# A chain of layers on one core: weight splits in halves and held back at norms, and a state-space stage whose inputs, skip term and Gelu are arranged anew

## The chip, the cores and the metric

The kernel runs on one core of a Trainium2 chip. The metric is the time on the device in microseconds (us), the median of several runs.

## What is computed

Two blocks of layers over 256 tokens of width 1024, all in float32. The first block has two layers: a mixer (a short convolution, then a dilated-window attention with rotary positions), a squared-ReLU MLP, and a gated projection of a side input ("ple"). The second block has two layers: a SwiGLU FFN ("ffn1"), a mixer (a state-space layer "S5", then a three-branch sparse attention), and a second SwiGLU FFN ("ffn2"); keys and values ("kv") for the sparse attention come from the first layer's output. Every part begins with an RMS norm. The state-space layer is the part that the change speaks of most:

```python
_, _, x_re, x_im = lax.associative_scan(combine, (la_re, la_im, bu_re, bu_im), axis=1)
y = (jnp.einsum('bsgp,ghp->bsgh', x_re, c_re) - jnp.einsum('bsgp,ghp->bsgh', x_im, c_im)
     + d_skip * ug)
y = jax.nn.gelu(y.reshape(bsz, seq, D_MODEL))
return y * jax.nn.sigmoid(y @ w_glu)
```

Here `ug` is the normed input in 64 groups of 16 channels, and the state of a group has 64 complex numbers.

## The kernel before

All activations lie transposed, with channels on the 128 partitions and the 256 tokens along the free axis, as 8 slices of 128 channels (`h0` to `h3` hold two each). The weights stream from memory in pieces of 128x2048 float32 (`raw`, 1 MB). A float32 product is made of three matmuls (`mm3`, L333 to L335): ScalarE copies the weights to a rounded high part (`whi`, L267), VectorE subtracts it from them (`wlo`, L271), and TensorE adds up high*high, low*high and high*low. Activations are split the same way (`xh` on ScalarE, `xl` on VectorE). A piece is split in two instructions of 128x1024 on either engine.

`piece` hands out the pieces in the order of a plan. Each call splits up to the piece `ahead` = 3 places on and loads three more. Whole tiles of the pool `ring`, three each of `raw`, `whi` and `wlo`, hold them.

A norm is not waited for: TensorE begins the layer's first pieces on the unscaled input (times the gain), one slice of channels after the other as `h` is written, three pieces at a time. Meanwhile the steps of the norm (`norm_at`, `norm_step`, a list `todo`) run: the mean of squares by a matmul, its power -0.5 (`rmean`, `rcol`), a diagonal `dg`, and a matmul of `dg` with ones (`norm_bc`, L509) whose result ScalarE copies to `R` (L511), the factors along the free axis. The results of the first pieces are multiplied by `R` when they are read (`e0`, L516). With three pieces under way, a fourth one, D, is the next that TensorE begins after them. `when_scaled` and the list `late` hold back what needs `R`; a scheduler sets the rest of the order, except that code under `in_order` is tied to the place where it is written.

The S5 stage (L1130 to L1310) goes by a written sequence, `S5_SEQ`: `r` puts the input rows in a grouped layout, `w` makes the state inputs of a quarter of the groups, `c` is the recurrence of a quarter (products on VectorE and GpSimd, a scan L1223 on VectorE, a rotation back, the states `sX` L1230), `t` and `o` apply two further tables (`to`, the short-range taps, and `wo`, the states), `R` turns half of the results back into channel slices and splits them, `K` (`skip`) multiplies the skip input `XG` by `R` on GpSimd (L1254, 8 instructions). The tables were computed in the background of earlier layers (`s5_taps`, `s5_tables`). ScalarE has already scaled `XG` by the skip weights (L1279). The result of `t` and `o` is copied to `UP` (L1163); at `R` VectorE adds `XG` to the transposed result (L1268), and ScalarE applies Gelu (L1272). After it come the matmuls of `w_glu`, a sigmoid (L1298), a product and the sum with `h` (L1299, L1300). Four pieces of weights in and after the stage (`BY_POOL`) have their low parts made on GpSimd (L269) instead of VectorE.

Of the kernel before, what the change touches and what calls it, by code (L numbers as in the profile page):

```python
# [10 lines left out]
F32 = mybir.dt.float32  # L11
# [6 lines left out]
D = 1024  # L18
# [30 lines left out]
SC_HEAD = SC_D + KT  # L49
# [6 lines left out]
S5_SEQ = "r0 r1 w0 r2 w1 r3 c0 w2 t0 c1 o0 w3 t1 t2 T o1 c2 t3 K o2 c3 R0 o3 R1 S"  # L56
# [143 lines left out]

BY_POOL = {S5_AT + S5_N + i for i in range(4)}
# [9 lines left out]
IN_ORDER = {E.DVE, E.Activation, E.Pool, E.PE}  # L211


class Ker:
    def __init__(self, ctx, tc, a):
# [13 lines left out]
        self.by_pool = BY_POOL  # L229
# [3 lines left out]
    def load(self, i):  # L233
        nc = self.nc
        while self.n_load < min(i, len(PLAN)):
            n, e = self.n_load, PLAN[self.n_load]
            if e[0] == "s5":

                m = (n - S5_AT) % 3
                t = self.ring.tile([128, NP_], F32R if m else F32, name=("raw", "whi", "wlo")[m])  # L240
                t = t.bitcast(F32) if m else t
                nc.sync.dma_start(t, self.s5w[e[1:]])
# [14 lines left out]
    def split(self, i):  # L257
        nc = self.nc
        while self.n_split < min(i, len(PLAN)):
            n = self.n_split  # L260
            assert PLAN[n][0] != "s5"
            self.load(n + 1)
            r = self.raw.pop(n)
            hi = self.ring.tile([128, NP_], F32R, name="whi")
            lo = self.ring.tile([128, NP_], F32R, name="wlo")
            for c in (slice(i, i + 1024) for i in range(0, NP_, 1024)):
                nc.scalar.activation(hi[:, c], r[:, c], AF.Copy)  # L267
                if n in self.by_pool:
                    nc.gpsimd.tensor_tensor(lo[:, c], r[:, c], hi[:, c].bitcast(F32), op=OP.subtract)  # L269
                else:  # L270
                    nc.vector.tensor_sub(lo[:, c], r[:, c], hi[:, c].bitcast(F32))  # L271
            self.spl[n] = (hi, lo)
            self.n_split += 1

    def piece(self, *want, ahead=3):
# [3 lines left out]
        if 0 <= d < S5_N:  # L279
# [3 lines left out]
            self.split(S5_AT + S5_N + max(0, (d - 3) // 3))  # L283
            self.n_use += 1
            return self.raw.pop(i)
        self.split(min(i + ahead, self.cap))
        self.load(i + ahead + 3 if d >= 0 or i + ahead < S5_AT else min(S5_AT + 3 * (i + ahead - S5_AT) + 3, S5_AT + 9))
# [8 lines left out]
    def step(self):  # L296
# [3 lines left out]
        while self.credit >= 1.0:  # L300
# [20 lines left out]

    def flush(self):
        self.credit = 0.0
        while self.bg:
            self.step()
# [11 lines left out]
    def cols_open(self, *want, ahead=3, ps="acc"):  # L337
        wh, wl = (w.rearrange("p (k c) -> p k c", k=KT) for w in self.piece("cols", *want, ahead=ahead))
        return self.psum(ps).rearrange("p (o t) -> p o t", o=2), wh, wl

    def cols_part(self, x, a, ks):
        acc, wh, wl = a
        for k in ks:
            for o in range(2):
                s = slice(128 * o, 128 * o + 128)
                self.mm3(acc[:, o], wh[:, k, s], wl[:, k, s], x[0][k], x[1][k],
# [1516 lines left out]
```

## Time and profile before

| | |
|---|---|
| median of 3 runs | 1875.27 us (1873.52 to 1877.62) |
| the profiled execution | 1871.9 us, its span 1870.1 us, mean granted TensorE clock 0.989 |
| busy | TensorE 97%, VectorE 69%, ScalarE 50%, GpSimd 25% |
| DMA | 344.68 MB, 184 GB/s on average |

PE is TensorE, ACT ScalarE, DVE VectorE, POOL GpSimd, SP the queue of the loads. The span is the time from the first to the last instruction of the core in the profiled execution. A line such as `L509` is line 509 of the kernel before. The granted clock is TensorE's share of full speed; it has two levels, 2.4 GHz (1.00) and 1.2 GHz (0.50), so a mean between them tells how long the lower one held.

### The profile page before, as it was taken

To read this page: it belongs to the slowest core of one execution; us is meant where nothing else is said; L and a number is where in the kernel's file an instruction comes from. 1 tells how busy PE (TensorE), PEld (TensorE's weight loads), DVE (VectorE), ACT (ScalarE), POOL (GpSimd) and SP (SyncE) were. 2 spreads that over 40 slices of the span, in tenths; PEclk is the share of its full clock that TensorE was granted. 3 is DMA by queue.
4 is the path that set the end of the run, shared out by engine and by line. 5 is a ranking of instruction groups with operands and counts; after the bars stand their busy time and mean duration, and the time that the engine had idled before them with its cause. 6 is when DMAs were issued, how large, how long until landed. Compare 5 with 4: busy or idle time off the path is not lost.

```text
span 1870.1 us, 35822 instructions
## 1 busy us (share of the span) xinstructions
PE 1817.1 (97%) x15244; PEld 1792.0 (96%) x15244; DVE 1281.1 (69%) x1633; ACT 942.3 (50%) x1442; POOL 468.5 (25%) x392
## 2 busy tenths in 40 slices
PE   8999999999999999999999779999999999999999
PEld 8999999999999999999999779999999999899999
DVE  6889887888776867778555566555785556875554
ACT  4365556555444555466443455444565445764442
POOL 2120012564652311112010442101243113421110
PEclk9999999999999999999999979999999999999999
DMA  6455666443343576666555734755455453445452
GB/s 253 181 187 209 220 223 219 161 152 142 136 144 127 198 236 227 219 207 254 188 186 187 291 128 172 263 185 186 174 187 200 173 183 118 65 161 181 181 180 90
DMA packets 78927, 344.68 MB, mean 184 GB/s; under 512 B 8022, under 2 KB 34378, under 8 KB 41392
## 3 DMA queue, kind: packets, MB, share of 16 engines
q1 hardware_dynamic: 77616, 339.30, 52.4%
q0 software_dynamic: 1008, 2.91, 0.4%
q8 instruction: 119, 1.95, 0.4%
q14 instruction: 40, 0.33, 0.1%
q10 hardware_dynamic: 144, 0.20, 0.0%
HBM read 328.71 MB, written 17.86 MB: 185 GB/s over the span
## 4 chain that ended last, share of the span: by engine, by line
PE 81%; DVE 7%; POOL 4%; issue 3%; ACT 2%; DMA 1%; SPq 0%; POOLq 0%; ACTq 0%; DVEq 0%
PE acc L334 16%; PE acc L335 16%; PE acc L333 16%; PE big L333 9%; PE big L334 9%; PE big L335 9%; DVE wlo L271 3%; POOL qks L736 2%; POOL qkt L739 1%; PE acc L1690 1%; POOL qkc L738 1%; ACT whi L267 1%; DMA bias<-zb 1%; PE big L1673 1%; PE misc L485 0%
## 5 line engine op out<-in xcount | busy, mean ns | idle before, releaser
L267 ACT ACTIVATE whi<-raw 128x1024 fp32r<-128x1024 f32 x558 | 559.8, 1051 | 599.8 <-issue 360.9
L271 DVE TENSOR_TENSOR wlo<-raw,whi 128x1024 fp32r<-128x1024 f32 x550 | 698.7, 1305 | 224.5 <-ACT whi L267 223.9
L334 PE MATMUL acc<-xl,whi 128*128 128x256 f32 x2096 | 595.7, 285 | 3.6 <-DVE xl L460 3.0
L333 PE MATMUL acc<-xh,whi 128*128 128x256 f32 x2096 | 594.5, 285 | 4.5 <-ACT whi L410 2.3
L335 PE MATMUL acc<-xh,wlo 128*128 128x256 f32 x2096 | 595.8, 285 | 3.0 <-DVE wlo L411 2.8
L333 PEld LDWEIGHTS acc<-xh,whi 128*128 128x128 f32 x2096 | 403.2, 193 | 6.4 <-ACT whi L410 2.7
L335 PEld LDWEIGHTS acc<-xh,wlo 128*128 128x128 f32 x2096 | 403.8, 193 | 5.3 <-DVE wlo L411 3.4
L334 PEld LDWEIGHTS acc<-xl,whi 128*128 128x128 f32 x2096 | 403.8, 193 | 4.8 <-DVE xl L460 3.4
L334 PE MATMUL big<-hl,whi 128*128 128x256 f32 x1216 | 343.6, 283 | 0.0
L335 PE MATMUL big<-hh,wlo 128*128 128x256 f32 x1216 | 343.2, 283 | 0.0
L333 PE MATMUL big<-hh,whi 128*128 128x256 f32 x1216 | 341.1, 284 | 0.0
L334 PEld LDWEIGHTS big<-hl,whi 128*128 128x128 f32 x1216 | 232.8, 191 | 0.5 <-issue 0.5
L335 PEld LDWEIGHTS big<-hh,wlo 128*128 128x128 f32 x1216 | 232.7, 191 | 0.2 <-issue 0.2
L333 PEld LDWEIGHTS big<-hh,whi 128*128 128x128 f32 x1216 | 231.0, 191 | 1.9 <-issue 1.9
L855 POOL TENSOR_TENSOR e<-e,R 128x512 f32<-128x512 f32 x44 | 80.6, 1833 | 524.5 <-ACT e L854 524.5
L335 PE MATMUL acc<-yh,wlo 128*128 128x256 f32 x720 | 204.1, 285 | 1.2 <-DVE wlo L271 1.0
L334 PE MATMUL acc<-yl,whi 128*128 128x256 f32 x720 | 204.1, 286 | 1.0 <-DVE yl L460 0.6
L333 PE MATMUL acc<-yh,whi 128*128 128x256 f32 x720 | 203.0, 286 | 0.8 <-ACT yh L410 0.5
L334 PEld LDWEIGHTS acc<-yl,whi 128*128 128x128 f32 x720 | 138.7, 193 | 2.0 <-DVE yl L460 1.3
L335 PEld LDWEIGHTS acc<-yh,wlo 128*128 128x128 f32 x720 | 138.9, 193 | 1.7 <-DVE wlo L271 1.2
L333 PEld LDWEIGHTS acc<-yh,whi 128*128 128x128 f32 x720 | 138.1, 194 | 2.2 <-ACT yh L410 1.3
L516 DVE TENSOR_TENSOR e<-acc,R 128x512 f32<-128x512 f32 x54 | 36.9, 689 | 84.4 <-PE acc L335 84.1
(440 smaller groups left out, 2592.4 us busy)
## 6 DMA issues: line engine op xcount, KB each, us to landing
raw<-in_wst SPq DMA_DIRECT2D x277, 1024.0 KB, 4.9
s5wo<-b SPq DMA_DIRECT2D x8, 512.0 KB, 5.7
s5wi<-wi SPq DMA_DIRECT2D x16, 256.0 KB, 3.7
s5to<-s5k SPq DMA_DIRECT2D x32, 128.0 KB, 4.5
bias<-zb SPq DMA_DIRECT2D x16, 256.0 KB, 4.5
cbt<-zb SPq DMA_DIRECT2D x4, 900.0 KB, 6.5
raw<-s5to SPq DMA_DIRECT2D x3, 1024.0 KB, 4.8
raw<-in_wst SPq DMA_DIRECT2D x4, 512.0 KB, 7.9
```

What stands on the lines that cost most here:

```text
L267: nc.scalar.activation(hi[:, c], r[:, c], AF.Copy)
L271: nc.vector.tensor_sub(lo[:, c], r[:, c], hi[:, c].bitcast(F32))
L333: mm(out, lh, rh, start=first, stop=False, skip_group_check=True)
L334: mm(out, lh, rl, start=False, stop=False, skip_group_check=True)
L335: mm(out, ll, rh, start=False, stop=last, skip_group_check=True)
L516: self.nc.vector.tensor_tensor(t, acc, self.bc2(self.R), op=OP.mult)
L736: nc.gpsimd.tensor_tensor(s, s, bc(self.rS), op=OP.mult)
L738: nc.gpsimd.tensor_tensor(c, t[:32], bc(self.rC), op=OP.mult)
L739: nc.gpsimd.tensor_tensor(t[:32], c, s, op=OP.add)
L855: nc.gpsimd.tensor_tensor(T[i], T[i], self.bc2(self.R), op=OP.mult)
L1673: nc.tensor.transpose(tp[:, 128 * n:128 * n + 128], blocks[4 * i + n], self.ident)
L1690: nc.tensor.matmul(o[:, dst], w, t[lp][:, e, b, src], start=False, stop=(b == 1 and kb == 1 and i == 2), skip_group_check=True)
```

## The change

It has four parts.

1. **Halves.** `whi` and `wlo` become pairs of 128x1024 tiles with a buffer each, six of either (`Halves`), where there were three of 128x2048. Either half can be split and released by itself. `rows` goes over the halves one after the other.
2. **Ordered splits at norms.** While fewer than four steps of a norm are left in `todo`, and the next two pieces are split, `piece` does not split and load further. It puts that work on `late`, and it is done, tied to its place by `in_order`, when `norm_bc` has issued `R`. Background work (`step`) also waits while a norm has steps left.
3. **The S5 stage.** `XG` has a tile of its own instead of one in the pool that the FFN before uses. The skip weights are added to the diagonal of the taps in the background work, so `XG`, scaled or multiplied by `R`, isn't needed at the end: `K`, the scaling by ScalarE and the addition on VectorE go. ScalarE applies Gelu where it copies the results out of PSUM. Nothing is split on GpSimd any more: the first halves of three pieces of `w_glu` are split at `P`, before the last results, the second halves at `Q`, after them. The Gelu table is loaded earlier.
4. **Loads.** The S5 tables come in two transfers of 512 KB each. The small constants have a different layout for the skip weights.

```diff
-S5_SEQ = "r0 r1 w0 r2 w1 r3 c0 w2 t0 c1 o0 w3 t1 t2 T o1 c2 t3 K o2 c3 R0 o3 R1 S"
+S5_SEQ = "r0 r1 w0 r2 w1 r3 T c0 w2 t0 c1 o0 w3 t1 t2 o1 c2 t3 o2 c3 P R0 o3 R1 Q S"
...
+class Halves:
+    def __init__(self, pool, name):
+        self.t = [pool.tile([128, NP_ // 2], F32R, name=name, bufs=6) for _ in range(2)]
...
-            for c in (slice(i, i + 1024) for i in range(0, NP_, 1024)):
-                nc.scalar.activation(hi[:, c], r[:, c], AF.Copy)
-                if n in self.by_pool:
-                    nc.gpsimd.tensor_tensor(lo[:, c], r[:, c], hi[:, c].bitcast(F32), op=OP.subtract)
-                else:
-                    nc.vector.tensor_sub(lo[:, c], r[:, c], hi[:, c].bitcast(F32))
...
+    def split_half(self, todo, c):
+        nc = self.nc
+        for r, hi, lo in todo:
+            rc = r[:, NP_ // 2 * c:NP_ // 2 * (c + 1)]
+            nc.scalar.activation(hi.t[c], rc, AF.Copy)
+            nc.vector.tensor_sub(lo.t[c], rc, hi.t[c].bitcast(F32))
...
-        self.split(min(i + ahead, self.cap))
-        self.load(i + ahead + 3 if d >= 0 or i + ahead < S5_AT else min(S5_AT + 3 * (i + ahead - S5_AT) + 3, S5_AT + 9))
+
+        def fetch():
+            self.split(min(i + ahead, self.cap))
+            self.load(i + ahead + 3 if d >= 0 or i + ahead < S5_AT
+                      else min(S5_AT + 3 * (i + ahead - S5_AT) + 3, S5_AT + 9))
+
+        if 0 < len(self.todo) < 4 and self.n_split >= i + 2:
+
+            self.late.append(lambda: self.behind(fetch))
+        else:
+            fetch()
...
-        while self.credit >= 1.0:
+        while self.credit >= 1.0 and not self.todo:
...
+    def behind(self, fn):
+        with self.in_order():
+            fn()
...
+                dd = bp.tile([16, 8, 16], F32, name="dd", bufs=1)
+                gp.tensor_tensor(dd, self.ident[:16, None, :16].to_broadcast([16, 8, 16]),
+                                 self.small[:16, SC_D + g0:SC_D + g0 + 8, None].to_broadcast([16, 8, 16]), op=OP.mult)
+                gp.tensor_tensor(ksb[:, :, :16], ksb[:, :, :16], dd, op=OP.add)
...
-        XG = big("XG", [2, 8, 4, 32])
+        XG = self.XG
...
-                evac(0, YP[0][:, :, 4 * q + 2 * i:4 * q + 2 * i + 2].rearrange("p j g h -> p g j h"),
-                     y[:, 256 * i:256 * i + 256].rearrange("p (g j h) -> p g j h", j=8, h=16))
-
-
-        def skip():
-            self.norm_bc()
-            Ri = self.R.rearrange("p (c i) -> p i c", i=8)
-            for k in range(KT):
-                t = XG[:, k // 4, :, k % 4]
-                gp.tensor_tensor(t, t, Ri, op=OP.mult)
-
+                ac.activation(YP[0][:, :, 4 * q + 2 * i:4 * q + 2 * i + 2].rearrange("p j g h -> p g j h"),
+                              y[:, 256 * i:256 * i + 256].rearrange("p (g j h) -> p g j h", j=8, h=16),
+                              AF.Gelu_apprx_tanh)
+
+        def presplit(c):
+            with self.in_order():
+                if c == 0:
+                    split.extend(self.split_open(3))
+                self.split_half(split, c)
...
-                v.tensor_tensor(dst[:, 4 * jb:4 * jb + 4], tp.rearrange("p (j g c) -> p j g c", j=4, c=32),
-                                XG[:, hf, 4 * jb:4 * jb + 4], op=OP.add)
-            for g in range(0, 4, 2):
-                k = 4 * hf + g
-                ac.activation(Y[0][:, k:k + 2], Y[0][:, k:k + 2], AF.Gelu_apprx_tanh)
-                for k in (k, k + 1):
-                    self.hilo(Y[0][:, k], x[0][k], x[1][k])
-
-        with self.in_order():
-            for k in range(KT):
-                t = XG[:, k // 4, :, k % 4]
-                ac.activation(t, t, AF.Copy, scale=self.small[:, SC_D + k:SC_D + k + 1])
+                evac(1 - jb, dst[:, 4 * jb:4 * jb + 4], tp.rearrange("p (j g c) -> p j g c", j=4, c=32))
+            for k in range(4 * hf, 4 * hf + 4):
+                self.hilo(Y[0][:, k], x[0][k], x[1][k])
...
+            self.XG = self.pp.tile([128, 2, 8, 4, 32], F32, name="XG", bufs=1)
```

How the second part moves instructions shows at the norm ahead of ffn2 in the first layer. ScalarE's queue from the table load on, before (`x2` is two instructions of the same piece; `e2` at L854 is the silu, `hh` a split of its product):

```order
L405 ACTIVATE tab_12958<-ones_76 128x1
L267 ACTIVATE whi_13028<-raw_12857 128x1024 x2
L847 ACTIVATE e2_13026<-acc_12968 128x512
L267 ACTIVATE whi_13101<-raw_12859 128x1024 x2
L267 ACTIVATE whi_13163<-raw_12966 128x1024 x2
L511 ACTIVATE R_13053<-misc_13051 128x256
L854 ACTIVATE e2_13057<-e0_13055 128x512
L854 ACTIVATE e2_13160<-e0_13158 128x512
```

and in the changed kernel:

```order
L433 ACTIVATE tab_13314<-ones_76 128x1
L875 ACTIVATE e2_13384<-acc_13326 128x512
L539 ACTIVATE R_13403<-misc_13401 128x256
L882 ACTIVATE e2_13407<-e0_13405 128x512
L289 ACTIVATE whi_13410<-raw_13213 128x1024
L289 ACTIVATE whi_13411<-raw_13213 128x1024
L289 ACTIVATE whi_13461<-raw_13215 128x1024
L289 ACTIVATE whi_13462<-raw_13215 128x1024
L289 ACTIVATE whi_13525<-raw_13324 128x1024
L289 ACTIVATE whi_13526<-raw_13324 128x1024
L882 ACTIVATE e2_13522<-e0_13520 128x512
```

The splits of D (`whi_13028` before, `whi_13410` and `whi_13411` now) and of the two pieces after it stood ahead of the copy of `R`, and now stand behind it and behind the first silu.

TensorE's queue at the same place, before (`misc<-dg,ones` is the matmul of `norm_bc`, L509 before and L537 after; `acc_13171` is D's result):

```order
L335 MATMUL acc_13109<-xh7_12661,wlo_12961 128x256
L333 MATMUL acc_13171<-xh0_12654,whi_13028 128x256
L509 MATMUL misc_13051<-dg_13049,ones_76 128x256
L334 MATMUL acc_13171<-xl0_12662,whi_13028 128x256
L335 MATMUL acc_13171<-xh0_12654,wlo_13029 128x256
```

and in the changed kernel, where `acc_13535` is D's result:

```order
L362 MATMUL acc_13471<-xh7_13017,whi_13317 128x256
L537 MATMUL misc_13401<-dg_13399,ones_76 128x256
L363 MATMUL acc_13471<-xl7_13025,whi_13317 128x256
L364 MATMUL acc_13471<-xh7_13017,wlo_13319 128x256
L362 MATMUL acc_13471<-xh7_13017,whi_13317 128x256
L363 MATMUL acc_13471<-xl7_13025,whi_13317 128x256
L364 MATMUL acc_13471<-xh7_13017,wlo_13319 128x256
L362 MATMUL acc_13535<-xh0_13010,whi_13410 128x256
L363 MATMUL acc_13535<-xl0_13018,whi_13410 128x256
L364 MATMUL acc_13535<-xh0_13010,wlo_13412 128x256
```

D was begun one matmul ahead of `norm_bc`, and is now begun in the sixth row behind it.

GpSimd's queue in the S5 stage, before (`sZ` is the sum that a scan starts from):

```order
L506 TENSOR_TENSOR dg_12530<-cst_112,rcol_12162 128x256
L1254 TENSOR_TENSOR XG_12131<-XG_12131,R_12534 128x8x32 x8
L1222 TENSOR_TENSOR sZ_12298<-sZ_12298,sZs_12299 128x512
L1222 TENSOR_TENSOR sZ_12364<-sZ_12364,sZs_12365 128x512
L1226 TENSOR_TENSOR sw_12300<-sw_12300,tC_11355 128x512
L1226 TENSOR_TENSOR sw_12366<-sw_12366,tC_11355 128x512
L1222 TENSOR_TENSOR sZ_12492<-sZ_12492,sZs_12493 128x512
L269 TENSOR_TENSOR wlo_12422<-raw_12379,whi_12421 128x1024 x2
L1222 TENSOR_TENSOR sZ_12574<-sZ_12574,sZs_12575 128x512
L269 TENSOR_TENSOR wlo_12509<-raw_12444,whi_12508 128x1024 x2
L269 TENSOR_TENSOR wlo_12671<-raw_12544,whi_12670 128x1024 x2
```

and in the changed kernel:

```order
L503 TENSOR_TENSOR rcol_12512<-rmean_12510,mhalf_78 128x2
L1256 TENSOR_TENSOR sZ_12647<-sZ_12647,sZs_12648 128x512
L1256 TENSOR_TENSOR sZ_12717<-sZ_12717,sZs_12718 128x512
L1260 TENSOR_TENSOR sw_12649<-sw_12649,tC_11686 128x512
L1260 TENSOR_TENSOR sw_12719<-sw_12719,tC_11686 128x512
L1256 TENSOR_TENSOR sZ_12848<-sZ_12848,sZs_12849 128x512
L1256 TENSOR_TENSOR sZ_12910<-sZ_12910,sZs_12911 128x512
```

The eight products with `R` and the low parts of the weights are gone from GpSimd; the low parts are VectorE's now.

## Rows read from the trace of the kernel before

**Rows 1.** The page, section 1: busy time of each engine, its share of the span.

```profile
PE 1817.1 (97%) x15244; PEld 1792.0 (96%) x15244; DVE 1281.1 (69%) x1633; ACT 942.3 (50%) x1442; POOL 468.5 (25%) x392
```

**Rows 2.** Stretches: length, busy PE, PEld, DVE, ACT, POOL; PEclk, DMA share, GB/s.

```profile
841.00:853.00 12.00, 12.00 (x101) 11.95 (x100) 11.19 (x16) 9.57 (x17) 1.30 (x1) 1.00 0.67 249
1028.00:1075.00 47.00, 36.12 (x499) 33.34 (x497) 27.32 (x36) 22.55 (x41) 22.72 (x23) 0.94 0.76 295
1075.00:1122.00 47.00, 36.89 (x318) 34.20 (x319) 30.45 (x34) 25.67 (x45) 20.95 (x11) 0.79 0.35 127
1139.50:1151.70 12.20, 12.20 (x102) 12.14 (x102) 9.28 (x12) 6.71 (x9) 3.65 (x4) 1.00 0.64 233
```

**Rows 3.** The chain of waits through the S5 stage: start, us, what.

```profile
1044.07 5.32 ACT XG L1148 x8
...
1054.46 0.68 PE misc L509 x2
...
1055.63 6.64 POOL XG L1254 x8
...
1063.55 2.28 DVE sw L1223
...
1108.81 0.49 ACT sZ L1298
...
1119.92 0.39 PE acc L334
```

**Rows 4.** The timeline of DVE in the S5 stage: start, us, engine, line, operation, out<-in.

```profile
1058.74 0.68 DVE L1221 TENSOR_TENSOR sZs<-acc,tS 128x512 f32<-128x512 f32 x1
...
1069.64 1.78 DVE L1227 TENSOR_TENSOR sws<-sws,tS 128x512 f32<-128x512 f32 x1
...
1072.54 2.85 DVE L1230 TENSOR_TENSOR sX<-sw,sws 128x512 f32<-128x512 f32 x1
1075.32 3.38 DVE L1223 TENSOR_TENSOR_SCAN sw<-tD,sZ 128x512 f32<-128x512 f32 x1
...
1091.20 0.69 DVE L1230 TENSOR_TENSOR sX<-sw,sws 128x512 f32<-128x512 f32 x1
...
1109.32 1.58 DVE L1299 TENSOR_TENSOR sZ<-sZ,ush 128x512 f32<-128x512 f32 x1 [6.00 <-ACT sZ L1298]
1110.93 2.79 DVE L1300 TENSOR_TENSOR h<-h,sZ 128x512 f32<-128x512 f32 x1
```

**Rows 5.** The timeline of POOL in the S5 stage.

```profile
1069.40 1.47 POOL L1226 TENSOR_TENSOR sw<-sw,tC 128x512 f32<-128x512 f32 x1 [0.40 <-ACT sws L1225]
...
1072.51 5.11 POOL L269 TENSOR_TENSOR wlo<-raw,whi 128x1024 fp32r<-128x1024 f32 x2
```

**Rows 6.** Waits of PE, whole program: engine line <- releaser: total us, times, longest.

```profile
PE big L789 <- ACT p L784: 9.6, 4, 2.5
...
PE acc L333 <- DVE e L625: 2.1, 1, 2.1
...
PE big L334 <- DVE ql L411: 1.2, 1, 1.2
```

**Rows 7.** Groups of instructions: line engine op out<-in xcount | busy, mean ns | idle before.

```profile
L267 ACT ACTIVATE whi<-raw 128x1024 fp32r<-128x1024 f32 x558 | 559.8, 1051 | 599.8 <-issue 360.9
...
L516 DVE TENSOR_TENSOR e<-acc,R 128x512 f32<-128x512 f32 x54 | 36.9, 689 | 84.4 <-PE acc L335 84.1
...
L854 ACT ACTIVATE e<-e 128x512 f32<-128x512 f32 x44 | 27.3, 621 | 9.0 <-DVE e L516 8.9
```

**Rows 8.** Timelines: DVE at the norm of ffn2, POOL at the attention's entry.

```profile
1140.60 2.36 DVE L271 TENSOR_TENSOR wlo<-raw,whi 128x1024 fp32r<-128x1024 f32 x2 [0.40 <-ACT whi L267]
...
351.94 1.30 POOL L736 TENSOR_TENSOR qks<-qks,rS 32x512 f32<-32x512 f32 x1
```

**Rows 9.** Stretches around waits of PE, columns as in rows 2.

```profile
380.00:388.00 8.00, 5.70 (x49) 5.50 (x48) 6.32 (x8) 4.76 (x9) 6.31 (x4) 1.00 0.36 131
...
635.00:643.00 8.00, 5.89 (x37) 5.69 (x36) 8.00 (x13) 4.27 (x6) 2.63 (x1) 0.79 0.69 262
```

## What the change should do to the time

> **What bounds the kernel now.** I read the page's busy times first: PE works for 1817.1 of 1870.1 us [rows 1], so the change can only give back what PE waits for or does at half clock. The stretches show where that is [rows 2]. Through the S5 stage PE works 36.12 and 36.89 of two times 47 us, at granted clocks of 0.94 and 0.79. At the norms there is nothing to give back: PE works 12.00 of 12.00 us at the ple norm of the second layer and 12.20 of 12.20 at the norm of ffn2, at full clock, 101 matmuls in 12.00 us, so one starts every 0.12. Third, the chain of waits through the S5 stage [rows 3] and what DVE and POOL do meanwhile [rows 4, 5]. A difference of 0.2%, 3.75 us, is about what a measurement can tell from none.
>
> **The S5 stage: about -12.** *Entry.* `XG` is written from 1044.07 on, for 5.32 us, once the FFN's pool is free [rows 3]. With a tile of its own it follows the four sums with `h`, the last of which is written at about 1044.6, and is complete by some 1046.4 instead of 1049.4: -3.0. The first recurrence's `sZs` ends at 1058.74 + 0.68 = 1059.4 [rows 4], but its sum on POOL queues behind eight products with `R` (from 1055.63 for 6.64 us), so the scan starts only at 1063.55 [rows 3]. Without them the sum's 1.3 us follow at once: 1059.4 + 1.3 = 1060.7, so another -2.8. The scan starts at about 1057.8.
> *Recurrences.* DVE's steps are long while POOL splits weights (5.11 us for two from 1072.51 [rows 5]): `sX` takes 2.85 instead of 0.69, a scan 3.38 instead of about 1.2, an earlier product 1.78 instead of 0.69 [rows 4]. These are 2.2 + 2.2 + 1.1; the second pair on POOL does the same to a later `sX` and scan, which I put at another 3. POOL's splits are gone, so -8.5: the last `sX`, which ends at 1091.20 + 0.69 = 1091.9 [rows 4], ends at 1077.6.
> *What is late next.* The three low halves of `P` (1.18 each, half of 2.36 [rows 8]) now stand on DVE between the last `sX` and the first splits of the results, so `w_glu` starts at about 1077.6 + 3.5 + 0.5 = 1081.6. Its first three results need 144 matmuls, 17.3 us, and a last table product of 1.0: 1099.9, or 1100.5 with a little half clock; before, the first is read at 1108.81 [rows 3]. -8.2. Behind it `sZ` and `h` took 1.58 and 2.79 instead of 0.69 beside POOL's last pair [rows 4], -3.0, and single halves stand ahead of `xl` on DVE where pairs stood, about -0.9. Sum -12. Between: -6, if only the entry counts, and -17, if half clock goes as well.
> Row against rule: the long products beside POOL are not only those beside splits. The one at 1069.64 took 1.78 beside a rotation product of POOL that began at 1069.40 [rows 4, 5], and those products stay. The Trainium skill (SBUF — State Buffer, "Who interferes with whom") says that a VectorE instruction with two inputs in SBUF contends with a GpSimd instruction that reads SBUF, one of them blocking whole; the trace agrees in the three long rows. By that rule the three low halves of `P` can wait for POOL in their turn: an estimate, 3 x 1.1 to 1.5 from that row, is that the stage would give back some 4 us less.
>
> **The norms: about +24.** Before, D's split was done when `norm_bc` was issued. Now it stands behind `R` and what ScalarE and VectorE do first with it, while PE's rows up to D stay few. From the start of the matmul of `norm_bc`, `R` is there 1055.63 - 1054.46 = 1.1 us later [rows 3]; a multiplied result takes 0.69, a silu 0.62, a half's copy 1.05 [rows 7], its low part 1.18 [rows 8]. Counting along the queues of the changed kernel:
> - ffn2: `R` 1.1, result 1.8, silu 2.4, `whi` 3.5, `wlo` 4.7. PE reaches D after six rows (0.9, with the 0.24 of `norm_bc` itself) and `wlo` two rows later, 1.1. Wait 3.5.
> - kv: D comes three rows behind `norm_bc`, and the next piece two rows later; its `whi` is the third copy (1.1 + 3 x 1.05 = 4.3), D's `wlo` stands behind three results (1.1 + 3 x 0.69 + 1.18 = 4.4). Wait 3.7.
> - attention entry: D comes at row 32, 4.1 us. ScalarE first splits `qh0`, which needs two results, a shuffle and POOL's rotation of 1.3 a step [rows 8]; I get 6.6, then `whi` 7.6, and `wlo`, behind `ql` and another result on VectorE, 9.3. PE needs `wlo` at row 37. Wait 4.9, of which 1.2 is there now [rows 6].
> - ple of the second layer: ffn1 begins at row 79. Its first `xl` stands on VectorE behind eight low parts and seven results, sums and products: 1.1 + 8 x 1.18 + 7 x 0.69 + 0.4 = 15.8, PE needs it at row 82, 10.1. Wait 5.7.
> - ple of the first layer: the same with seven low parts, 14.6 against row 93, 11.4. Wait 3.2.
> - the convolution's norm and that of ffn1 in the first layer, by the same count, 2.4 and 1.9; both mlp norms and the last norm have over 40 rows of cover: 0.1 in all.
> Together 25.4, less 1.2: +24. The cover was D's early split; what pays is PE, which has no idle time there to lose. Between +14, if copies and low parts overlap better than I counted, and +27.
>
> **mlp norm of the second layer: -4.** PE waits 2.1 there for a product of VectorE [rows 6], and the 8 us around it have a clock of 0.79 [rows 9], which is 8 x 0.21 = 1.7 lost. In the changed kernel the splits ahead of that product are behind it. Between -2 and -5.
>
> **Clock: +3.** A wait of PE is followed by a stretch at half clock at times: after the one just named the mean is 0.79, after a wait for the softmax of the same length (four of them, 9.6 in all [rows 6]) it is 1.00 [rows 9]. Six of the new waits are as long. I take two falls at 1.7; none, and six, are the ends.
>
> **At nothing:** halves that come free sooner (ScalarE and VectorE work ahead of PE wherever it is dense), the row order, Gelu in the copy (a copy was there), the taps' two small products per group of eight (POOL is busy 25% [rows 1], and they lie in the mlp's background), twelve more loads on SP, the added split of `PT` chunks in the sparse attention. If their covers failed, each costs under 2 us.
>
> **Sum.** -12 + 24 - 4 + 3 = +11 against the profiled execution's 1871.9, so 1882.9. The median of the runs is 3.4 above that execution: 1886.
>
> **Rivals.**
> - *The S5 stage pays for the norms* (faster, 0.27). PE's idle time there is 47 - 36.12 + 47 - 36.89 = 21 us, and at half clock another 47 x 0.06 + 47 x 0.21 = 12.7 are lost, part of them in the idle time. If the presplit halves let `w_glu` run at full clock directly behind the recurrences, and PE's way into the stage closes up too, it can give back 22 to 26; the point is where it exceeds the norms' 20 to 24. For it: the entry and the recurrences alone are 14 on DVE. Against it: three low parts now stand on the path. Time: 1875 - 24 - 4 + 20 = 1867.
> - *They cancel* (0.13). S5 -16, norms +20, mlp -4, no clock: 1875. That is also the time if the deferral bites less than its rows say, as at norms with many rows of cover.
> - *The clock falls after every long new wait* (0.14): six times 1.7 instead of two, and some of them twice: 1894. For it, rows 9 at 635; against it, 380.
> - *VectorE's new low parts queue with POOL's products* (0.08): S5 gives only 7, 1890. The rule quoted above is this one.
> - My forecast, 1886, has the remaining 0.38.
>
> **The numbers.** Slower holds my forecast and the last two rivals, 0.60; same 0.13; faster 0.27. The range runs from 1864 to 1898: below it only the S5 rival with cheap norms, above it only clock and port together. The forecast's own range is 1879 to 1893.
>
> **What the profile will show.** Right: at ffn2's norm PE waits about 3.5 us for a `whi` or `wlo` right behind `norm_bc`, 3.7 at kv, near 5 at the attention's entry and 5.7 at ffn1's entry, and ScalarE's copy of `R` starts 0.6 behind the matmul; the first scan starts 5.7 earlier in the stage, no step of VectorE there takes over 2 us, and the first result of `w_glu` is read 8 us earlier; the wait for L625's product is gone. Wrong: if PE is still dense at those norms, the step on the deferral has failed; if the S5 stage is over 18 us shorter, its terms were too small; if the clock falls behind each new wait, the time is in the 1890s.

## The result, and the profile after

The changed kernel takes 1886.89 us (median of 5 runs, 1882.22 to 1887.48), the kernel before 1875.33 in the same comparison (1873.52 to 1877.62): a ratio of 1.0061, with a 95% interval of 1.0050 to 1.0072. It is slower by 0.6%. The profiled execution took 1886.62 us, its span is 1884.8 us, its mean granted clock 0.984. In the changed kernel a copy to `whi` is L289, a low part L290, the matmul of `norm_bc` L537 and a result times `R` L544.

The page, section 1, of the changed kernel, beside [rows 1]:

```profile
PE 1826.6 (97%) x15242; PEld 1800.5 (96%) x15242; DVE 1292.8 (69%) x1647; ACT 956.5 (51%) x1438; POOL 465.3 (25%) x391
```

Stretches of the changed kernel, columns as in [rows 2]: the ple norm of the second layer, two through the S5 stage, the norm of ffn2, and kv:

```profile
847.00:871.00 24.00, 18.58 (x133) 18.12 (x132) 22.86 (x32) 18.34 (x35) 1.69 (x1) 0.86 0.48 176
1050.00:1097.00 47.00, 35.27 (x546) 30.84 (x544) 33.55 (x45) 24.04 (x44) 12.87 (x14) 0.89 0.71 250
1097.00:1126.00 29.00, 28.68 (x229) 28.58 (x229) 22.86 (x31) 20.57 (x32) 2.06 (x1) 0.94 0.56 218
1139.90:1152.10 12.20, 8.93 (x60) 8.46 (x59) 10.06 (x10) 8.48 (x11) 3.69 (x4) 0.86 0.36 136
1338.00:1350.20 12.20, 9.63 (x63) 9.13 (x63) 9.53 (x11) 8.07 (x9) 0.78 (x2) 0.86 0.51 175
```

At ffn2's norm PE works 8.93 of 12.20 us and issues 60 matmuls, where it worked all of 12.20 and issued 102 [rows 2]. In the S5 stage PE is nearly dense from 1097 on: 28.68 of 29.00. (The S5 stretches here and in [rows 2] aren't cut at the same places of the program; the table below compares like with like.)

What PE waits for in the changed kernel, whole program (total us, times, longest):

```profile
PE big L817 <- ACT p L812: 7.6, 4, 2.8
PE big L362 <- ACT whi L289: 5.7, 3, 3.1
PE acc L362 <- ACT xh L441: 3.6, 1, 3.6
...
PE acc L362 <- ACT whi L289: 2.6, 2, 2.3
PE acc L362 <- DVE e L544: 2.4, 1, 2.4
...
PE acc L364 <- DVE wlo L290: 2.1, 2, 1.1
PE misc L1104 <- DVE b L1125: 1.8, 2, 1.0
...
PE acc L363 <- DVE xl L442: 1.8, 1, 1.8
```

Of [rows 6] the softmax waits are still there, the 2.1 for the product L625 is gone, and the waits for `whi`, `wlo`, `xh` and `xl` at norms are new. They sit at the places that the prediction named, except the convolution's norm.

Where the time went can be read by numbering the 13752 weight matmuls (those of `mm3`), which are as many in both kernels, and taking the start of the same number in either trace:

| weight matmul | what ends there | before, us | after, us | after - before | step |
|---|---|---|---|---|---|
| 2460 | convolution and first mlp | 316.2 | 317.4 | +1.2 | +1.2 |
| 2640 | ple norm, first layer | 339.7 | 346.2 | +6.4 | +5.2 |
| 3660 | attention's entry and its first half | 474.8 | 486.3 | +11.5 | +5.0 |
| 4830 | rest of the attention | 628.8 | 638.2 | +9.4 | -2.1 |
| 5040 | mlp norm, second layer | 659.3 | 663.8 | +4.5 | -4.9 |
| 6360 | second mlp | 828.7 | 834.9 | +6.1 | +1.7 |
| 6660 | ple norm, second layer | 868.6 | 882.1 | +13.6 | +7.4 |
| 6780 | norm of ffn1 | 883.9 | 898.9 | +15.0 | +1.5 |
| 8340 | ffn1 and S5 | 1125.6 | 1126.6 | +1.0 | -14.0 |
| 8610 | norm of ffn2 | 1160.4 | 1166.7 | +6.2 | +5.2 |
| 10080 | kv | 1338.1 | 1349.0 | +10.9 | +4.7 |
| 13751 | sparse attention to the end | 1865.6 | 1880.0 | +14.5 | +3.6 |

The six norms cost 29.0 us (ple, attention, ple, ffn1, ffn2, kv), the S5 stage gives back 14.0. Of the -2.1 in the attention, 1.5 is in two waits of PE for low parts (2.1 before, 0.6 now); the +1.7 in the second mlp is in no longer wait that the profile lists, and stays unexplained.

Now ffn2's norm in the timeline of the changed kernel. PE, where two matmuls of a `x2` are written as one row:

```profile
1139.88 0.59 PE L537 MATMUL misc<-dg,ones 128*128 128x256 f32 x2
...
1140.78 0.28 PE L364 MATMUL acc<-xh,wlo 128*128 128x256 f32 x1
1143.35 0.38 PE L362 MATMUL acc<-xh,whi 128*128 128x256 f32 x1 [2.29 <-ACT whi L289]
1143.57 0.28 PE L363 MATMUL acc<-xl,whi 128*128 128x256 f32 x1
1144.84 0.58 PE L364 MATMUL acc<-xh,wlo 128*128 128x256 f32 x1 [0.98 <-DVE wlo L290]
```

ACT there:

```profile
1140.51 0.38 ACT L539 ACTIVATE R<-misc 128x256 f32<-128x256 f32 x1 [5.82 <-PE misc L537]
1141.72 0.63 ACT L882 ACTIVATE e<-e 128x512 f32<-128x512 f32 x1 [0.83 <-DVE e L544]
1142.25 5.77 ACT L289 ACTIVATE whi<-raw 128x1024 fp32r<-128x1024 f32 x6
```

DVE there:

```profile
1141.60 0.68 DVE L544 TENSOR_TENSOR e<-acc,R 128x512 f32<-128x512 f32 x1
1143.33 1.45 DVE L290 TENSOR_TENSOR wlo<-raw,whi 128x1024 fp32r<-128x1024 f32 x1 [1.04 <-ACT whi L289]
```

ScalarE idles for 5.82 us ahead of `R`, where its queue had the copies of three pieces before; the six copies follow in a row once the silu is done. Behind `norm_bc` PE has five rows left, the last of which starts at 1140.78, and then it waits 2.29 for the first copy and 0.98 for its low part.

### The profile page after: what moved, and what is told of

Its sections match the earlier page's. It is cut to its first block, busy times and chain, and to the rows that moved or that the text cites. A ratio compares the mean times of both kernels' runs of the same rounds, so it can differ in the third digit from the quotient of the medians.

```text
span 1884.8 us, 36094 instructions
## 1 busy us (share of the span) xinstructions
PE 1826.6 (97%) x15242; PEld 1800.5 (96%) x15242; DVE 1292.8 (69%) x1647; ACT 956.5 (51%) x1438; POOL 465.3 (25%) x391
## 4 chain that ended last, share of the span: by engine, by line
PE 77%; DVE 8%; POOL 5%; issue 4%; ACT 3%; DMA 2%; SPq 0%; POOLq 0%; ACTq 0%; DVEq 0%
PE acc L364 15%; PE acc L363 15%; PE acc L362 15%; PE big L364 8%; PE big L363 8%; PE big L362 8%; DVE wlo L290 3%; POOL qkt L767 2%; POOL qks L764 2%; ACT whi L289 1%; POOL qkc L766 1%; PE acc L1720 1%; DMA bias<-zb 1%; DMA s5wi<-wi 1%; ACT qh L438 1%
## 5 line engine op out<-in xcount | busy, mean ns | idle before, releaser
L290 DVE TENSOR_TENSOR wlo<-raw,whi 128x1024 fp32r<-128x1024 f32 x558 | 709.4, 1282 | 312.4 <-ACT whi L289 309.1
L289 ACT ACTIVATE whi<-raw 128x1024 fp32r<-128x1024 f32 x558 | 581.2, 1056 | 540.5 <-PE acc L363 279.6
L883 POOL TENSOR_TENSOR e<-e,R 128x512 f32<-128x512 f32 x44 | 74.0, 1682 | 554.0 <-ACT e L882 544.9
L482 POOL TENSOR_TENSOR sq<-sq,sqt 128x512 f32<-128x512 f32 x27 | 42.0, 1554 | 138.5 <-ACT sqt L481 137.9
```

The source lines that it names most:

```text
L289: nc.scalar.activation(hi.t[c], rc, AF.Copy)
L290: nc.vector.tensor_sub(lo.t[c], rc, hi.t[c].bitcast(F32))
L482: nc.gpsimd.tensor_tensor(self.sq, self.sq, s, op=OP.add)
L883: nc.gpsimd.tensor_tensor(T[i], T[i], self.bc2(self.R), op=OP.mult)
```

## The experiments

**Theory A** is the prediction's: the splits held back behind `R` make PE wait, the S5 stage gives back part of it. **Theory B**: the half buffers make the splits late, held or not. Numbers in the next paragraphs are ratios to the kernel before on the same chip, with their 95% intervals.

### No holding, holding alone, halves alone, holding at the mlp norms

The first kernel takes the change's second part out:

```diff
-        if 0 < len(self.todo) < 4 and self.n_split >= i + 2:
-            self.late.append(lambda: self.behind(fetch))
-        else:
-            fetch()
+        fetch()
...
-        while self.credit >= 1.0 and not self.todo:
+        while self.credit >= 1.0:
```

> The changed kernel, with the splits and loads never held back at a norm, and the background work going on there (the change's second part taken out). Theory A (the held splits cost the time): the waits of PE behind norm_bc go (some 19 us, and 8 to 10 of half clock behind them), the wait of 2.1 for the product L625 in the second mlp comes back with its half clock (4): 1887 - 28 + 4 = 1863, 12 us under the kernel before, all of it in the S5 stage. Theory B (the half buffers make the splits late, whether held or not): the waits stay, about 1880 to 1887.

Measured: 1855.22 us, 0.9909 (0.9896 to 0.9923) of the kernel before, and so 1.5% under the changed kernel: the second part costs 28 to 32 us (1886.89 - 1855.22 = 31.7, but the kernel before took 1875.33 beside the one and 1872.79 beside the other; by the two ratios 1.0061 - 0.9909 = 0.0152 of 1875, 28.5). Stretches of this kernel: the ple norm of the second layer, ffn2's norm and kv:

```profile
831.00:855.00 24.00, 24.00 (x200) 23.89 (x199) 22.69 (x31) 19.52 (x37) 2.14 (x1) 1.00 0.47 170
1119.00:1131.20 12.20, 12.20 (x102) 12.15 (x101) 9.86 (x12) 6.19 (x9) 4.29 (x4) 1.00 0.59 203
1315.00:1327.20 12.20, 12.20 (x104) 12.20 (x103) 7.58 (x10) 4.81 (x6) 0.78 (x2) 1.00 0.63 231
```

PE is dense again, at full clock. Theory B falls for these norms. Two things were not expected: the wait for L625's product did not come back, which is 4 of the 8 us by which this kernel is faster than 1863, and PE has one new wait, at ffn1's norm (its list of waits):

```profile
PE acc L358 <- ACT e L878: 3.1, 1, 3.1
```

All eight kernels here with half buffers that don't hold at that norm have this wait, of 3.1 or 3.2 us, the one with the first part alone too; the kernel before has none there. So the first part has a price of its own at one norm. In four of the eight profiles 3.4 us of half clock followed this same wait, in the other four none.

The second kernel is the kernel before with the second part alone:

```diff
-        self.split(min(i + ahead, self.cap))
-        self.load(...)
+        def fetch():
+            self.split(min(i + ahead, self.cap))
+            self.load(...)
+        if 0 < len(self.todo) < 4 and self.n_split >= i + 2:
+            self.late.append(lambda: self.behind(fetch))
+        else:
+            fetch()
...
+        while self.credit >= 1.0 and not self.todo:
```

> The kernel before, with the second part of the change alone: splits and loads held back at norms, whole buffers, the old S5 stage. Theory A: the same waits as in the changed kernel, and the gain at the second mlp norm: 1875 + 28 - 4 = 1899, between 1893 and 1903. Theory B: 1875, within 3.

Measured: 1907.45 us, 1.0185 (1.0171 to 1.0199): +34.7 us, more than in the changed kernel. Its list of waits:

```profile
PE big L802 <- ACT p L797: 13.0, 4, 5.7
PE big L346 <- ACT whi L267: 9.3, 3, 6.7
PE acc L346 <- ACT whi L267: 6.3, 3, 2.8
```

The longest, 6.7 for a `whi`, is the one at the attention's entry, and a softmax wait behind it grew to 5.7. In the changed kernel the longest of either kind are 3.1 and 2.8, so half buffers soften the holding; they don't cause these waits. Theory A's direction holds, its number was 8 us short, outside the 1893 to 1903. At the second mlp norm this kernel gains as the prediction said: its list has no wait for the product (L638 here), and the numbered matmuls gain 3.7 from 4830 to 5040. The product comes right behind `R` on DVE, ahead of the low parts:

```profile
650.34 1.29 DVE L638 SCALAR_TENSOR_TENSOR e<-acc,R 128x512 f32<-128x512 f32 x2 [4.86 <-ACT R L524]
```

The third kernel has the half buffers, the order of `rows` and the two transfers per table, and nothing else of the change: no holding, the S5 stage of before with `XG`, `K` and the low parts on GpSimd:

```diff
-            hi = self.ring.tile([128, NP_], F32R, name="whi")
-            lo = self.ring.tile([128, NP_], F32R, name="wlo")
+            self.spl[n] = tuple(Halves(self.ring, w) for w in ("whi", "wlo"))
...
+        fetch()
...
-        for o in outs:
-            for k in range(2):
+        for k, o in ([(k, o) for o in outs for k in range(2)] if last else [(k, o) for k in range(2) for o in outs]):
```

> The kernel before with the first part and the loads of the fourth alone: half buffers, rows over the halves, the tables in two transfers; no holding back, the old S5 stage. Theory A: 1875, within 3, PE dense at the norms. Theory B: 1890 or more, with PE's waits behind norm_bc.

Measured: 1869.42 us, 0.9981 (0.9972 to 0.9990), faster by 0.2%, and so a little more than the expected "within 3". At 600 to 650 us PE has no wait for L625's product. The timeline of DVE in this kernel, where the product is L653:

```profile
631.21 1.23 DVE L293 TENSOR_TENSOR wlo<-raw,whi 128x1024 fp32r<-128x1024 f32 x1 [0.70 <-ACT whi L292]
...
635.75 1.27 DVE L653 SCALAR_TENSOR_TENSOR e<-acc,R 128x512 f32<-128x512 f32 x2
```

and in the kernel before:

```profile
631.07 4.41 DVE L271 TENSOR_TENSOR wlo<-raw,whi 128x1024 fp32r<-128x1024 f32 x2 [2.23 <-ACT whi L267]
...
638.68 1.28 DVE L625 SCALAR_TENSOR_TENSOR e<-acc,R 128x512 f32<-128x512 f32 x2
```

Before, a low-part pair of 4.41 and another of 2.35 stood ahead of the product; with halves, fewer stand there. So the first part removes this wait without any holding, as the holding did without the first part. Of the first part, half buffers and the order of `rows` were not tried apart. Its gain of 3.4 us is a sum: by the numbered matmuls of this trace the mlp norm gives 3.4 and the ffn1 norm takes 5.7, and this was one of the slower executions. From this kernel to the one without holding is the S5 part alone: 0.9909 - 0.9981, 1869.42 - 1855.22 = 14.2 us (11.3 between matmuls 6780 and 8340 of their two traces).

The fourth kernel holds splits and background work back at the two mlp norms alone:

```diff
-        if 0 < len(self.todo) < 4 and self.n_split >= i + 2:
+        if self.hold and 0 < len(self.todo) < 4 and self.n_split >= i + 2:
...
-        while self.credit >= 1.0 and not self.todo:
+        while self.credit >= 1.0 and not (self.hold and self.todo):
```

`hold` is set at the head of `mlp` and cleared ahead of `ple_proj`.

> The changed kernel, with splits held back at the two mlp norms alone, where over 40 rows lie between norm_bc and the fourth piece. Theory A: 1863 as without holding, less the 4 of the second mlp's wait and its half clock: 1859. Theory B: about 1880.

Measured: 1858.77 us, 0.9924 (0.9910 to 0.9938): not 4 less than without holding, but 3.5 more, with intervals that overlap. The number fits the expected 1859, for the wrong reason: the gain that it was to keep was there already. In the trace the numbered matmuls fall behind those of the kernel without holding by 2.4 between 278 and 291 us, of which 1.9 stays; its waits there are

```profile
PE misc L1107 <- DVE b L1128: 1.8, 2, 1.0
```

for the state-space tables of the background work. The changed kernel has the same two waits.

### The terms of the S5 stage

Three kernels put one suspected cost each back into the kernel without holding. The first adds GpSimd work beside the last recurrences:

```diff
             gp.tensor_tensor(Z, Z, Zs, op=OP.add)
+            if q > 1:
+                a = XG[:, 0].rearrange("p (e i) g c -> p e (i g c)", e=2)
+                for k in range(2):
+                    gp.tensor_tensor(a, a, Z[:, None, :].to_broadcast([128, 2, 512]), op=OP.subtract)
```

> The kernel without holding (1855.2), with four added subtractions of 128x1024 on GpSimd behind the sums of the last two recurrences, as long as the low parts that the kernel before made there; what they write is read by nobody. If the low parts on GpSimd were what made VectorE's steps of the recurrences long (the prediction's 8.5 us), steps of 0.7 to 1.2 grow to 1.8 to 3.4 again and the time rises by 4 to 8 us: 1859 to 1863. If the steps were long for another reason, 1855 within 2.

Measured: 1866.11 us, 0.9961 (0.9947 to 0.9974), +10.9, above the expected 1859 to 1863. GpSimd and then DVE in this kernel:

```profile
1072.75 8.29 POOL L1256 TENSOR_TENSOR XG<-XG,sZ 128x1024 f32<-128x1024 f32 x3
```

```profile
1073.22 2.84 DVE L1261 TENSOR_TENSOR sws<-sws,tS 128x512 f32<-128x512 f32 x1
...
1076.90 1.92 DVE L1264 TENSOR_TENSOR sX<-sw,sws 128x512 f32<-128x512 f32 x1
1078.75 3.37 DVE L1257 TENSOR_TENSOR_SCAN sw<-tD,sZ 128x512 f32<-128x512 f32 x1
```

Without the added work these three take 0.68, 0.68 and 1.21 there. The numbered matmuls fall 6.7 behind through the stage (weight matmuls 6800 to 8200), which is within the 4 to 8 that were expected, and part of it is clock: half clock lasts 23.9 us there (from 1067.8), and 13.7 without the added work. About 2.4 more come later, up to number 12000, where this trace has 10.2 us at half clock in the sparse attention from 1583.3 on, and the rest lay ahead of the stage.

The second puts eight GpSimd products back ahead of the first recurrence's sum:

```diff
+            if q == 0:
+                Ri = Rs[:, :8, None].to_broadcast([128, 8, 32])
+                for k in range(KT):
+                    t = XG[:, k // 4, :, k % 4]
+                    gp.tensor_tensor(t, t, Ri, op=OP.mult)
             gp.tensor_tensor(Z, Z, Zs, op=OP.add)
```

> The kernel without holding (1855.2), with eight products of 128x256 on GpSimd on XG, which is read no more, ahead of the first recurrence's sum, where the kernel before multiplied XG by R. The prediction's term: the products delay the sum and the scan by about 2.8, so 1858. If the sum has slack: 1855 within 1.

Measured: 1857.27 us, 0.9914 (0.9901 to 0.9928), the same as without them. POOL in this kernel:

```profile
1050.44 4.63 POOL L1256 TENSOR_TENSOR XG<-XG,Rs 128x256 f32<-128x256 f32 x8 [1.35 <-DVE Rs L1211]
1057.22 1.27 POOL L1257 TENSOR_TENSOR sZ<-sZ,sZs 128x512 f32<-128x512 f32 x1 [2.15 <-DVE sZs L1251]
```

The products are over 2.15 us before the sum's input is there. They took `Rs`, which is ready before `R` was; the kernel before began them at 1055.63 for 6.64 us [rows 3], with its sum's input ready at 1059.4. So eight products don't delay the sum by themselves; a late factor and the longer 6.64 were part of that term. How much each had is not tried.

The third puts `XG` into the stage's own pool again:

```diff
-        XG = self.XG
+        XG = big("XG", [2, 8, 4, 32])
```

> The kernel without holding (1855.2), with XG in the stage's own pool again, whose space the FFN before holds until its end. The prediction's term: XG is complete 3.0 us later, all behind it too, so 1858. If the copies of h were late for another reason: 1855 within 1.

Measured: 1858.84 us, 0.9929 (0.9909 to 0.9948), an interval that overlaps both expectations. ACT in this kernel:

```profile
1040.35 5.29 ACT L1177 ACTIVATE XG<-h,small 128x256 f32<-128x256 f32 x8 [10.13 <-PE big L360]
```

Counted from the first square on GpSimd (1034.58 without holding, 1036.67 here), `Rs` comes after 12.85 instead of 10.89, 2.0 later, but the first scan after 19.55 instead of 19.11, only 0.4 later. Both kernels have 3.4 us of half clock there: with the early `XG` it falls behind `Rs` (1046.1 to 1049.5), on the products that lead to the scan, and here ahead of it (1045.3 to 1048.7). So neither the 2.0 nor the 0.4 is the place of `XG` alone. Through the stage the numbered matmuls lose 0.5.

### What is held, and what else can be moved

The first kernel here goes after the new wait of 3.1 at ffn1's norm, by moving one step of that norm:

> The kernel without holding (1855.2), where PE waits 3.15 us at ffn1's norm in the first layer for a result that R multiplies: there all three accumulators are taken. The step norm_bc is put one norm step sooner at this norm alone. If R is ready sooner by the 1.4 us of that step, the wait falls to about 1.7 and the time to 1854; if the diagonal is late instead, 1855.

```diff
-                self.norm_at((ssq, N1), (bc, N2))
+                self.norm_at((ssq, N1), (bc, N2 - 1))
```

Measured: 1857.08 us, 0.9919 (0.9906 to 0.9933); the wait is 3.1 as before. The matmul of `norm_bc` still stands right ahead of the row that waits, as in the kernel without holding, so the step that was to come sooner did not. This attempt settles nothing about the diagonal.

The next kernel makes the splits at once and holds only the loads:

```diff
-        def fetch():
-            self.split(min(i + ahead, self.cap))
+        def fetch():
             self.load(...)
         if 0 < len(self.todo) < 4 and self.n_split >= i + 2:
+            self.split(min(i + ahead, self.cap))
             self.late.append(lambda: self.behind(fetch))
         else:
+            self.split(min(i + ahead, self.cap))
             fetch()
...
-        while self.credit >= 1.0 and not self.todo:
+        while self.credit >= 1.0:
```

> The changed kernel with its splits made at once, as without holding, and only the loads that go with them held back until R; background work goes on. If the place of the splits on ScalarE and VectorE is the cost: as without holding, 1855 within 3, PE dense behind norm_bc at ffn2 and kv. If what costs is that the raw pieces are loaded later: most of the 31 us stay, 1875 or more.

Measured: 1857.03 us, 0.9913 (0.9897 to 0.9930). ACT at ffn2's norm in this kernel:

```profile
1119.61 2.01 ACT L289 ACTIVATE whi<-raw 128x1024 fp32r<-128x1024 f32 x2 [0.66 <-PE acc L364]
1123.16 0.38 ACT L540 ACTIVATE R<-misc 128x256 f32<-128x256 f32 x1 [1.54 <-PE misc L538]
1123.63 1.06 ACT L289 ACTIVATE whi<-raw 128x1024 fp32r<-128x1024 f32 x1
```

The copies stand ahead of `R` again, and the cost is gone. It is the splits' place, not the loads'.

The last kernel is the changed one with its background work not held (`while self.credit >= 1.0:`).

> The changed kernel, its splits and loads held back at all norms, but the background work not. Holding at the mlp norms with the background work held cost 2.2 in two waits for the state-space tables (at 273 and 289 us). If the held background work makes these, they go: 1885. The waits behind norm_bc stay as in the changed kernel: 2.4, 3.1, 5.4, 1.5, 3.4 and 2.7.

Measured: 1885.04 us, 1.0061 (1.0046 to 1.0076), the changed kernel's ratio. The two waits for the tables are gone, but the waits at the ple norm of the first layer are 2.9 and 2.8 instead of 2.4 and 0.3, since the order there changed too. What the held background work costs by itself is not separated: nothing in the total, up to 2.4 at the first mlp norm.

Taken out one after the other, the parts are: halves -0.2%, the S5 stage -0.7%, holding +1.5%. That they make the measured +0.6% follows from how they were taken, as steps between the same kernels, and shows nothing. The independent figure is holding alone on the kernel before, +1.85%: with whole buffers it costs more, so the parts don't simply add up. The kernel without holding beats both: 1855.22 us, 0.9909 of the kernel before.

## Why the prediction came out right

1886 was forecast, within 1864 to 1898, and 1886.89 was measured. The mechanism was right: held splits make PE wait at the norms that were named, and the S5 stage gives back less than that. That the number came out within 1 us is luck: of the terms, the waits were 6 us too dear, the clock 8 too cheap and the S5 stage 2 too small, and the +3.6 of the sparse attention was not forecast. The +11 was counted against the profiled execution, and between the two profiled executions it is +14.7 (1886.62 - 1871.9); the 3.4 by which the median was put above the profile is 0.3 in the changed kernel, which hides most of that.

**The waits at the norms: mechanism right, +24 forecast, +18 measured.** Forecast and measured by norm: ffn2 3.5 and 3.3 (2.29 + 0.98, above); kv 3.7 and 2.6; attention's entry 4.9 and 4.1; ple of the second layer 5.7 and 5.4 (3.6 for `xh`, 1.8 for `xl`); ffn1 1.9 and 1.4; ple of the first layer 3.2 and 2.7; the convolution's norm 2.4 and nothing. Together 19.5, less the 1.2 of [rows 6]. What was mis-sized is the step that counts along the queues by means of single instructions: six copies in a row took 5.77, 0.96 each, not 1.05, and three results at kv took 1.9 (1338.99 to 1340.87), not 2.07. At the convolution's norm, with its long row of small steps, that error probably used up the whole wait, though the prediction doesn't show that count: D's low part was done 10.9 us after `norm_bc`, against 10.7 at which PE wanted it. That the fourth piece's early split was the cover is shown by the two kernels in which it is back (no holding, and only loads held): dense stretches, and 28 to 32 us less.

**The clock: +3 forecast, about +11 measured.** This is the term that was most mis-sized. The six norms cost 29.0 by the numbered matmuls, and 18.3 of these are waits, which leaves 10.7. Behind five of these norms the clock was halved for 3.4, 6.8, 6.8, 3.4 and 3.4 us, 23.8 in all, which can cost up to 11.9; so the rest fits half clock. Stretches of the changed kernel behind the waits at the attention's entry, the ple norm of the second layer and kv, and in the sparse attention:

```profile
356.00:364.00 8.00, 6.97 (x35) 6.59 (x35) 8.00 (x7) 4.81 (x6) 6.03 (x4) 0.57 0.32 110
861.00:869.00 8.00, 6.19 (x34) 5.99 (x33) 8.00 (x15) 6.41 (x17) 0.00 (x0) 0.57 0.62 246
...
1342.00:1350.00 8.00, 8.00 (x54) 7.97 (x55) 6.31 (x8) 4.45 (x5) 0.00 (x0) 0.79 0.77 261
1600.00:1613.00 13.00, 11.45 (x46) 9.90 (x46) 9.12 (x27) 8.36 (x30) 6.04 (x14) 0.61 0.30 54
```

The clock fell behind five of the six norms with long waits, for 6.8 us at two of them (a mean of 0.57 over 8 us), where two falls that cost 1.7 each were forecast. The rival that has it fall behind every one was the truer picture of this term; it gave 1894 only because the waits and the S5 stage were taken too dear beside it. The fourth row is not a norm: there the sparse attention waits for a bias by DMA as it did before, and in this execution, and in one more of those profiled, half clock follows, 3.6 us in the table. The mean clock of the runs (0.982 to 0.988, and 1882.22 us for the one at 0.988) says that such stretches come and go.

**The S5 stage: -12 forecast, -14.0 measured.** By its steps, counted from the last matmul of the FFN (1043.62 before, 1058.66 after). DVE, ACT and PE in the changed kernel:

```profile
1073.07 1.22 DVE L1257 TENSOR_TENSOR_SCAN sw<-tD,sZ 128x512 f32<-128x512 f32 x1 [1.39 <-POOL sZ L1256]
...
1075.64 1.74 DVE L1261 TENSOR_TENSOR sws<-sws,tS 128x512 f32<-128x512 f32 x1 [0.16 <-ACT sws L1259]
1077.30 2.29 DVE L1257 TENSOR_TENSOR_SCAN sw<-tD,sZ 128x512 f32<-128x512 f32 x1
...
1093.44 0.69 DVE L1264 TENSOR_TENSOR sX<-sw,sws 128x512 f32<-128x512 f32 x1
1094.05 3.49 DVE L290 TENSOR_TENSOR wlo<-raw,whi 128x1024 fp32r<-128x1024 f32 x3
...
1112.45 0.69 DVE L1326 TENSOR_TENSOR sZ<-sZ,ush 128x512 f32<-128x512 f32 x1
```

```profile
1111.05 0.60 ACT L1325 ACTIVATE sZ<-acc 128x512 f32<-128x512 f32 x1
```

```profile
1096.10 1.01 PE L362 MATMUL acc<-yh,whi 128*128 128x256 f32 x3
```

- *Entry*: the scan starts at 14.4 instead of 19.9 (1063.55 in [rows 3]): -5.5, forecast -5.8. How it splits between `XG` and the products was forecast 3.0 and 2.8; the two experiments give each less than that alone, so the parts overlap, or hang on `R` being late, and that split stays open.
- *Recurrences*: from the first scan to the last `sX` 20.4 instead of 27.65 ([rows 4]): -7.3, forecast -8.5. The cause is shown: added GpSimd work makes the same kinds of steps long again. The missing 1.2 fits steps of 1.74 and 2.29 beside the products that stay on GpSimd; the 2.29 also misses the sign that no step there takes over 2 us.
- *Behind the recurrences*: here the forecast failed, twice. The three low halves were to put the first result of `w_glu` 6 us later relative to the last `sX`; it is read 17.6 us behind it before (1091.20 to 1108.81) and 17.6 now. The halves do take 3.49, but `w_glu` begins 2.7 behind the start of that `sX` (4.7 by the working), and 99 weight matmuls, not 144, stand between its start at 1096.10 and the reading of the first result at 1111.05, some 15 us with half clock until 1100.2 in them, where 18.3 were counted. So, counted from the last matmul of the FFN, the first result is read 12.8 sooner, not 8.2. Behind it 3.9 more was forecast, and 1.2 is left of the 14.0: `sZ` and `h` do take 0.69 and 0.68 now, but low parts stand ahead of them on DVE (`sZ` comes only at 1112.45, behind a pair from 1110.17).
- *The rule of the Trainium skill that the prediction quoted* (SBUF — State Buffer, "Who interferes with whom"): the low halves took 3.49 for three, no longer than the 1.18 each of [rows 8]; GpSimd had no work there (none from 1087.66 to 1122). So the rival by which they queue did not occur, and these rows don't test the rule; that VectorE's steps are long beside GpSimd's is measured with the added GpSimd work above.

**The mlp norm of the second layer: -4 forecast, -4.9 measured.** The step "the splits ahead of that product are behind it" is right: holding alone removes the wait (-3.7). But the first part alone removes it too (-3.4), though its halves stood at nothing in the sum, so this gain can be had without the holding's price.

**At nothing** stood the halves. Alone they make -3.4 (1869.42 against 1872.79), net of a gain at that mlp norm and a loss at ffn1's norm. The held background work makes two waits of 1 us at 273 and 289 us, part of the +1.2 in the table's first row, but nothing that shows in the total (1885.04 without it).

## What to carry to other kernels

Work that an engine does while it waits is free only as long as it stands ahead of the wait in its queue: an ordered hold behind a late result (here `R`) turns 1 us of copies per half piece into waits of the engine that has no slack, and behind five of the six norms half clock came with them. Before holding work back, count for each place how many rows of the bound engine lie between the release and the first use of what is held; where only the fourth piece hung on it, 40 rows and more lost nothing, D in the third or the sixth row about 3 us. And take a change of several parts apart, each part alone on the kernel before as well: here one part's +1.5% hid two that gave -0.9%, and one wait was removed twice over.

## What was not expected

- A VectorE step of 0.68 to 1.21 us took 1.9 to 3.4 beside a GpSimd subtraction of 128x1024, and the whole stage lost 6.7 us to 11 us of such work that nobody waited for, some of it by a longer stretch at half clock.
- Half clock cost at the norms over half as much again as the waits (10.7 beside 18.3 us), and it followed even two waits of 1.2 and 1.4 us at kv. But the same wait of 3.1 at ffn1's norm was followed by half clock in four kernels and not in four others, so a wait's length alone doesn't tell.
- Holding loads alone cost nothing that shows (1857.03 against 1855.22, intervals overlapping).
